# Placing the context branch among the expert weights by order edges on TensorE, and norming the second context at the end of the mixer

## The chip, the cores and the metric

The kernel runs on one core of a Trainium2 chip, in float32 (large products by three passes over a split of the operands). The metric is the device time of one launch in microseconds (us), as a median of runs. The profile is one further execution, with every instruction recorded.

## The reference

Two blocks of two layers each, on a latent sequence x and a context, both 256 tokens of width 1024. The first block mixes the context and the latents (heads with a scan, a convolution, a Fourier mix) and runs 16 experts behind each mixer; the second layer of it does both for the latents alone. The second block starts with a Hyena layer on both sequences and ends with attention on the latents over latents and context. Cut to what the change touches:

```python
# first block, last layer (l = 1): latents only
x = x + gt1 * (mix_x @ w_out[l])
x = x + gt2 * expert_choice_ffn(modulated_rmsnorm(x, g_norm2[l], sh2, sc2), ...)   # 16 experts, 32 tokens each
# second block, layer 0
h_ctx = rms_norm(ctx_2, norm_g) * (1 + sc_c) + sh_c          # needs nothing of the first block
proj = h_ctx @ w_in                                          # 1024 x 8192, four parts: x0, x1, v, z
x0, x1, v = short_conv(proj[..., :6144])                     # width 3
u = x1 * v
y = irfft(rfft(u, 512) * rfft(k, 512))[:256]                 # long convolution, done as products with DFT matrices
x_ctx = ctx_2 + gt_c * (((y + u * d) * x0 * silu(z)) @ w_out)   # 2048 x 1024
```

So the context's Hyena branch of the second block depends on nothing that the second layer's experts compute, and the two can run side by side.

## The kernel before, in words

**Order.** The program is written as one stream of tile operations, and a scheduler with a simulated timeline (`schedule_with_timeline_sim=True` in `build`) fixes the order of the instructions of each engine ahead of the run. An engine then works through its list in order and waits where an operand or a buffer is not ready. What is written in parallel (the experts and the context branch) is interleaved by that scheduler, by the times that it simulates.

**Queues.** SP issues nearly all weight loads: tiles of 128x2048 (1.05 MB) into the tag W with 5 buffers. In `run` the context branch has a ring of its own, the tag Wb with 2 buffers, and its loads are issued by POOL for the first 15 of its 16 tiles (the blocks `(0, 4), (4, 4), (8, 4), (12, 3)`), and by SP for the sixteenth (`[(15, 1)]`), which waits for expert 14 (`self.late[14]`).

**The second layer, in order.** `mixer(1, ...)` ends with the heads' loop (L582 to L608), the Fourier mix (L644), the convolution's norm (L666 to L673) and the output projection: `loadN` (L320) loads w_out in four loads of four k-blocks, `projN_steps` splits each k-block into hi (L104, ScalarE) and lo (L105, VectorE) and multiplies in three passes (L109 to L111). `ada` computes the adaLN vectors, tile by tile: a load (L186), and for each eight matmuls into the bank `pad` (L191). Which adaLN tiles are computed where is the table `PLACES`: in "L1" they are mixed into the heads' loop, one step after every head step (`beside`), in "R1" they come in `route_tokens`, ahead of the gathering of the experts' tokens (L798). The tiles "a1 b0 b1" are the three last groups of the second block's two layers: 16 loads.

**The experts.** `experts` runs for each of 16 experts over gate, up and down weights: each is four tiles of two k-blocks (`ew`, L895), and each k-block is one `expert_k` (L823), with the stationary operand the 32 gathered tokens (XS) or the hidden values (hT) and the weights streaming through. The four quarters of a k-block's 1024 columns go to four groups of 32 rows of the array: 3 x 8 x 4 matmuls for each expert. Between up and down lie ScalarE (L851), VectorE (L854), a transpose (L857) and its copy (hT). VectorE weights the result (L869), and every fourth expert it is scattered back by matmuls (L875). The first six weight tiles go to a tag of their own, W2 (6 buffers; `r = 11 - self.ecount`), all others to W, so that eleven can be loaded ahead of the first expert.

**The context branch.** `hyena` handles 128 channels at a time: for each of the four parts one load of 128x1024x2 and one `projT` of eight k-blocks, split in halves of four (hi, lo in 2 buffers, `sbufs`), 24 matmuls of 256 columns for each. VectorE and ScalarE form the short convolution, POOL folds u into sums and differences (L1058), TensorE transposes them (L1059), goes through the DFT matrix fe and, after VectorE's product with the kernel's spectrum Kt (L1077), back through fi (L1017). The results hm feed `out_proj`, in blocks of four tiles. Before, the context is loaded, its adaLN row and column formed and the normed transposes hyx made at the place where the branch begins, behind the call of `experts`.

In what follows a *piece* is a projection's half: four k-blocks of one `projT`, or one k-block of `out_proj`. The branch's first 15 tiles make 120 + 30 = 150 pieces.

Of the kernel before, what the change touches and what calls it, by code (L numbers as in the profile page):

```python
# [22 lines left out]

SB = 4
# [3 lines left out]
PLACES = dict(P0="", M0="01 02 10", L0="", R0="a0", W1="", P1="11", M1="12", L1="", R1="a1 b0 b1")  # L28
# [3 lines left out]
class K:  # L32
    def __init__(self, ctx, tc, A, out):
# [14 lines left out]
        self.side, self.turn = (None, 1), 0  # L48
        self.wgate, self.late = [], {}

# [56 lines left out]
    def mm3(self, out, l, r, start, stop):  # L107
        mm = self.nc.tensor.matmul
        mm(out, lhsT=l[0], rhs=r[0], start=start, stop=False)  # L109
        mm(out, lhsT=l[0], rhs=r[1], start=False, stop=False)  # L110
        mm(out, lhsT=l[1], rhs=r[0], start=False, stop=stop)  # L111

# [153 lines left out]
    def projT(self, ps, w, x, c0, n):  # L266
        for k0 in range(0, 8, 4):
# [58 lines left out]
    def mixer(self, l, x, hc, cols, R, ada):  # L326
# [8 lines left out]
        with self.pool("nrm", tags=("xh", "xtmp")):  # L335
            for s, src in ((0, hc), (1, x)):
                xh = self.normed(src, "og" if s else "xh", 1)
# [7 lines left out]
        ott = [0, 1, 2, 3] if full else [2, 3]  # L345
        cum = []
# [5 lines left out]
        wg = {}  # L352
# [72 lines left out]
        flo = T([128, 2, 2, 128], "flo")  # L425
        for s in streams:
# [14 lines left out]
            if s in om:  # L441
                Q[s] = self.parts([128, 1, 256], "Q", 2, True)
# [5 lines left out]
            if s in om:  # L448
# [3 lines left out]
                nc.scalar.activation(flo[:, s], pm, AF.Exp, scale=-1.0)  # L452
# [19 lines left out]
        sgc = T([128, 2, 512], "t4k", 2)  # L472
        ypad = T([128, 2, 2, 286], "ypad")
        nc.vector.memset(ypad[:, :, :, 0:15], 0.0)
        nc.vector.memset(ypad[:, :, :, 271:286], 0.0)
        for h in range(2):
            ps = self.P([128, 512])
            self.projT(ps[:, oc0:], chunk(1 + h), X, oc0, on)
            nc.scalar.activation(sgc[:, h, oc0:], ps[:, oc0:], AF.Sigmoid)
        for h in range(2):  # L480
            ps = self.P([128, 512])
            self.projT(ps[:, oc0:], chunk(3 + h), X, oc0, on)
            for s in om:
                nc.vector.tensor_tensor(ypad[:, h, s, 15:271], ps[:, s * 256:s * 256 + 256],
                                        sgc[:, h, s * 256:s * 256 + 256], op=OP.mult)

        cw, cbias = self.colv["cw", l], self.colv["cb", l]
        acc = T([128, 2, 2, 256], "t4k", 2)
        yo = slice(0, 2) if full else slice(1, 2)

        def terms():
            for j in range(31):
                for h in range(2):
                    av, yv = acc[:, h, yo], ypad[:, h, yo, j:j + 256]
# [10 lines left out]
        qT = T([128, 4, 512], "qT")  # L505
# [4 lines left out]
        for h in range(4):  # L510
            ps = self.P([128, 512])
            self.projT(ps[:, oc0:], chunk(9 + h), X, oc0, on)
            self.copy(qT[:, h, oc0:], ps[:, oc0:])
# [9 lines left out]
        fz = T([128, 4, 256], "t4k", 2)  # L523
# [3 lines left out]
        for q, t in enumerate(ott):  # L527
            self.copy(fz[:, t], pss[q])


        og = T([128, 4, 512], "og")
# [3 lines left out]
        for q, t in enumerate(ott):  # L535
            nc.scalar.activation(og[:, t], pss[q], AF.Sigmoid)
            nc.vector.tensor_tensor(og[:, t], og[:, t], ghn, op=OP.mult)
# [32 lines left out]
        mhi = T([128, 8, 512], "mhi", 1, F32R)  # L570
        mlo = T([128, 8, 512], "mlo", 1, F32R)
# [4 lines left out]
        for s in om:  # L576
            hh[s] = T([128, 4, 2, 128], "hh", 2)
            for h in range(4):
                pS = self.P([128, 2, 256])
                c0 = s * 256  # L580
                for t in range(2):
                    nc.tensor.matmul(pS[:, t], lhsT=kT[:, h, c0 + t * 128:c0 + (t + 1) * 128], rhs=qT[:, h, c0:c0 + 256],  # L582
                                     start=True, stop=True)
                for d in range(2):
# [13 lines left out]
                    if s == 1:  # L598
# [5 lines left out]
                        nc.vector.tensor_tensor(qs, qs, qT[:, h, 256:512], op=OP.mult)  # L604
# [12 lines left out]
                    nc.vector.tensor_tensor(rd, rd, flo[:, s, :, r], op=OP.max)  # L617
# [10 lines left out]
            for h in range(4):  # L628
                pt = self.PT([128, 256])
                for t in range(2):  # L630
                    nc.vector.scalar_tensor_tensor(hh[s][:, h, t], hh[s][:, h, t], rsh[:, s, h, t:t + 1],
                                                   og[:, 2 * s + t, h * 128:(h + 1) * 128], op0=OP.mult, op1=OP.mult)
                    nc.tensor.transpose(pt[:, t * 128:(t + 1) * 128], hh[s][:, h, t], self.ident)
                c0 = s * 256
# [4 lines left out]
        for h in range(2):  # L639
            po = self.PT([128, 512])  # L640
            for s in om:
                ps = self.PS([128, 512])
                for t in range(2):
                    nc.tensor.matmul(ps, lhsT=fz[:, 2 * s + t, h * 128:(h + 1) * 128], rhs=fw[:, t], start=(t == 0), stop=(t == 1))  # L644
# [5 lines left out]
            nc.scalar.copy(mhi[:, 6 + h, oc0:], po[:, oc0:])  # L650
# [951 lines left out]
```

## Time and profile before

| | |
|---|---|
| median of 3 runs | 2360.59 us (2359.33 to 2368.23) |
| profiled execution | 2366.99 us, its span 2365.2 us |
| busy share of the span | PE 90%, PEld 61%, DVE 53%, ACT 31%, POOL 8% |
| mean granted clock of TensorE | 0.955 |
| DMA, mean over the span | 281 GB/s, 664.09 MB |

PE is TensorE's matmuls, PEld its weight loads beside them, DVE is VectorE, ACT ScalarE, POOL GpSimd, SP the engine that issues most loads. PEclk is the clock that TensorE was granted, as a share of full speed (2.4 GHz); 0.76 over a stretch is a mixture of the levels 2.4 and 1.2 GHz. TensorE's 90% is a mean over stages: a table of stretches tells in which of them DMA is the full resource and in which TensorE is. A line of waits names the instruction that stood, the last thing that it stood for, and the time; a line of SP's timeline with a long duration and few issues (54.33 us for 16) is SP standing at a load whose buffer is not free yet.

### The profile page before, as it was taken

What the parts mean: (1) busy time and instruction counts of PE and PEld (TensorE: products, weight loads), DVE (VectorE), ACT (ScalarE), POOL (GpSimd) and SP (SyncE); (2) the same over time, 40 slices, a digit from 0 to 9 for tenths busy, and PEclk for the clock granted to TensorE, in tenths of its full rate; (3) what the DMA queues carried; (4) which work ended last, traced back from release to release, by engine and by line L of the source; (5) the groups of instructions that cost most, each with busy time, mean ns of one, the idle gap of its engine ahead of it and who ended that gap; (6) DMA issues with size and microseconds to landing.
All of it is one profiled execution on the core that took longest, in us unless ns stands there. A gap on an engine that the chain in (4) does not pass through costs nothing.

```text
span 2365.2 us, 35049 instructions
## 1 busy us (share of the span) xinstructions
PE 2135.7 (90%) x13966; PEld 1436.1 (61%) x13966; DVE 1250.4 (53%) x2533; ACT 737.5 (31%) x1414; POOL 187.7 (8%) x315
## 2 busy tenths in 40 slices
PE   5999988999999989998799998898777999999998
PEld 3776664343343436864376766665234999979786
DVE  3954444333433337654355555544125878875776
ACT  3323331000000014343233222222013555555665
POOL 1000000011010100000011011100001110100100
PEclk8999999999999999999899999998777999999999
DMA  8247545999999996459799999988996545435320
GB/s 342 99 157 312 204 184 193 413 415 415 414 413 415 414 405 251 137 194 370 295 351 365 372 374 370 351 336 327 421 421 262 185 144 188 168 132 189 126 81 26
DMA packets 129588, 664.09 MB, mean 281 GB/s; under 512 B 12666, under 2 KB 23429, under 8 KB 62352
## 3 DMA queue, kind: packets, MB, share of 16 engines
q1 hardware_dynamic: 115616, 602.89, 66.0%
q0 software_dynamic: 13808, 58.96, 6.6%
q8 instruction: 110, 1.80, 0.3%
q14 instruction: 54, 0.44, 0.1%
HBM read 656.56 MB, written 5.24 MB: 280 GB/s over the span
## 4 chain that ended last, share of the span: by engine, by line
PE 72%; DVE 9%; issue 8%; DMA 7%; ACT 3%; POOL 1%; SPq 0%; DVEq 0%; POOLq 0%; ACTq 0%
PE pmm L823 16%; PE pmm L109 12%; PE pmm L111 11%; PE pmm L110 11%; PE pad L191 3%; PE psm L875 2%; DMA W<-in_w_e_gate 1%; DVE lo L105 1%; DMA W<-in_w_e_up 1%; PE ptp L1017 1%; DMA W<-in_w_ada 1%; PE pmm L798 1%; PE pad L978 1%; DMA W<-in_ada_w 1%; PE ppo L1247 1%
## 5 line engine op out<-in xcount | busy, mean ns | idle before, releaser
L823 PE MATMUL pmm<-W,XS 128*32 128x256 f32 (+1 forms) x3040 | 378.8, 478 | 39.7 <-DMA W<-in_w_e_gate 20.3
L105 DVE TENSOR_TENSOR lo<-W,hi 128x512 fp32r<-128x512 f32 (+1 forms) x420 | 283.7, 680 | 187.1 <-ACT hi L104 184.2
L104 ACT CAST hi<-W 128x512 fp32r<-128x512 f32 (+1 forms) x420 | 255.5, 612 | 352.0 <-PE pmm L110 162.9
L823 PEld LDWEIGHTS pmm<-W,XS 128*32 128x32 f32 (+1 forms) x3040 | 127.0, 123 | 241.3 <-issue 151.1
L823 PE MATMUL pmm<-W,hT 128*32 128x256 f32 (+1 forms) x1536 | 190.1, 483 | 20.2 <-DVE hT L101 8.3
L111 PE MATMUL pmm<-hyx,lo 128*128 128x256 f32 x640 | 191.6, 299 | 10.6 <-DVE lo L105 10.6
L109 PE MATMUL pmm<-hyx,hi 128*128 128x256 f32 x640 | 193.4, 302 | 4.8 <-ACT hi L104 4.8
L110 PE MATMUL pmm<-hyx,hi 128*128 128x256 f32 x640 | 185.8, 290 | 0.0
L105 DVE TENSOR_TENSOR lo<-Wb,hi 128x512 fp32r<-128x512 f32 x160 | 109.4, 692 | 117.3 <-ACT hi L104 116.3
L104 ACT CAST hi<-Wb 128x512 fp32r<-128x512 f32 x160 | 96.8, 619 | 209.4 <-PE pmm L110 138.3
L869 DVE TENSOR_TENSOR Y<-pmm,gt 32x512 f32<-32x512 f32 (+1 forms) x128 | 70.9, 554 | 143.5 <-PE pmm L823 141.8
L109 PE MATMUL pmm<-hyl,hi 128*128 128x256 f32 x512 | 144.5, 283 | 1.7 <-DVE rtmp L697 1.7
L110 PE MATMUL pmm<-hyl,hi 128*128 128x256 f32 x512 | 144.1, 282 | 0.0
L111 PE MATMUL pmm<-hyl,lo 128*128 128x256 f32 x512 | 143.1, 283 | 0.0
L109 PEld LDWEIGHTS pmm<-hyx,hi 128*128 128x128 f32 x640 | 126.6, 198 | 23.7 <-ACT hi L104 16.6
L111 PEld LDWEIGHTS pmm<-hyx,lo 128*128 128x128 f32 x640 | 126.3, 197 | 22.3 <-DVE lo L105 14.1
L823 PEld LDWEIGHTS pmm<-W,hT 128*32 128x32 f32 (+1 forms) x1536 | 65.6, 125 | 117.6 <-issue 68.6
L110 PEld LDWEIGHTS pmm<-hyx,hi 128*128 128x128 f32 x640 | 126.6, 198 | 2.4 <-issue 2.2
L851 ACT ACTIVATE h<-pmm 128x256 f32<-128x256 f32 (+1 forms) x31 | 15.1, 488 | 362.1 <-PE pmm L823 361.9
L191 PE MATMUL pad<-W,cpad 128*32 128x512 f32 x576 | 91.0, 643 | 21.6 <-DMA W<-in_w_ada 16.7
L854 DVE TENSOR_TENSOR h<-h,pmm 128x512 f32<-128x512 f32 (+1 forms) x32 | 17.7, 552 | 171.9 <-ACT h L851 89.5
L109 PEld LDWEIGHTS pmm<-hyl,hi 128*128 128x128 f32 x512 | 97.4, 190 | 3.4 <-issue 1.9
(516 smaller groups left out, 4084.1 us busy)
## 6 DMA issues: line engine op xcount, KB each, us to landing
W<-in_w_e_gate SPq DMA_DIRECT2D x128, 1024.0 KB, 11.2
W<-in_w_e_up SPq DMA_DIRECT2D x128, 1024.0 KB, 11.2
W<-in_w_e_down SPq DMA_DIRECT2D x128, 1024.0 KB, 11.2
W<-in_w_ada SPq DMA_DIRECT2D x48, 1024.0 KB, 6.6
W<-in_hyw SPq DMA_DIRECT2D x32, 1024.0 KB, 5.1
Wb<-in_hyw POOLq DMA_DIRECT2D x30, 1024.0 KB, 8.9
W<-in_ada_w SPq DMA_DIRECT2D x24, 1024.0 KB, 5.2
W<-in_at_w_in SPq DMA_DIRECT2D x16, 1024.0 KB, 5.0
```

Source lines behind the costliest of these rows:

```text
L104: self.nc.scalar.copy(hi, w)
L105: self.nc.vector.tensor_tensor(lo, w, hi.bitcast(F32), op=OP.subtract)
L109: mm(out, lhsT=l[0], rhs=r[0], start=start, stop=False)
L110: mm(out, lhsT=l[0], rhs=r[1], start=False, stop=False)
L111: mm(out, lhsT=l[1], rhs=r[0], start=False, stop=stop)
L191: nc.tensor.matmul(ps[32 * j:32 * j + 32, :], lhsT=self.cpad[:, blk, k0 + k, :], rhs=wt[:, k, j * 512:(j + 1) * 512], start=(k0 + k == 0), ...
L798: nc.tensor.matmul(ps, lhsT=v, rhs=S[s][:, t], start=(t == 0 and q == 0), stop=(t == 1 and q == 1))
L823: self.nc.tensor.matmul(ps[M * j:M * j + M], lhsT=v, rhs=wt[:, j * N:(j + 1) * N], start=(k == 0), stop=(k == 7))
L869: nc.vector.tensor_tensor(Y[s][32 * r:32 * r + 32, c], py[p0:p0 + 32], gt[s][p0:p0 + 32, c], op=OP.mult)
L875: nc.tensor.matmul(ps, lhsT=SgT[s][:, q, t * 128:(t + 1) * 128], rhs=Y[s][:, n * 512:(n + 1) * 512], start=True, stop=True)
L978: nc.tensor.matmul(ps[:, i, f], lhsT=self.fd[:, t, i * 256 + f * 128:i * 256 + (f + 1) * 128], rhs=ab[:, i, t], start=(t == 0), stop=(t == 1))
L1017: self.nc.tensor.matmul(out, lhsT=l[0], rhs=r[0], start=start, stop=stop)
```

## The change

Six edits, one diff:

1. **Order edges.** `place` adds an edge without a semaphore (it binds the scheduler's order on TensorE, and costs the run nothing) from the first matmul of a piece to an expert cluster. `self.clusters` lists, for the second layer, the last matmul of every second k-block of `expert_k`, that is one cluster for each weight tile, 12 for each expert. The k-th piece of the first 15 context tiles may issue only behind cluster int(1.2 k) - 4.
2. **adaLN.** "a1 b0 b1" go from "R1" (in `route_tokens`) to "L1" (beside the heads of the mixer, ahead of w_out).
3. **Second context.** `load_x("ctx_2")`, its adaLN column and `modulated` go from the start of the context branch to the end of the second mixer, with the pool x2 for its transposes.
4. **Experts of the second layer.** The down projection of expert e - 1 is written behind gate and up of expert e (`put_off`); W2 has 4 buffers for 6 and lies on the other side of the memory, so nine prefetch tiles in place of eleven.
5. **Context branch.** Four hi/lo buffers for two; the transposes of uf come a part later; the back end (inverse transform, product, `out_proj`) is written behind the next tile's third part (`pend`, `flush`); the inverse transform makes 128 columns for each half of the spectrum and forms the other 128 positions by a sum and a reversed difference on VectorE (`back`).
6. **Second mixer.** Tiles of the latents alone have half the width (`on` for 512, `len(om)`, `len(ott)`), and the banks of `ps0` are listed in another order.

```diff
+SHARE, LEAD = 1.2, 4
-PLACES = dict(P0="", M0="01 02 10", L0="", R0="a0", W1="", P1="11", M1="12", L1="", R1="a1 b0 b1")
+PLACES = dict(P0="", M0="01 02 10", L0="", R0="a0", W1="", P1="11", M1="12", L1="a1 b0 b1", R1="")
...
+    def place(self, first):
+
+        if self.mixed is None:
+            return
+        i = int(self.mixed * SHARE) - LEAD
+        self.mixed += 1
+        if 0 <= i < len(self.clusters):
+            self.tc.add_manual_dep(first.ins, self.clusters[i].ins.name,
+                                   mybir.DependencyInfo(mybir.DependencyClass.NoSync, mybir.DependencyReason.DATA),
+                                   reason="share")
...
                 kk = k0 + k
-                self.mm3(ps, (hi[:, k], lo[:, k]), (x[0][:, kk, c0:c0 + n], x[1][:, kk, c0:c0 + n]), kk == 0, kk == 7)
+                first = self.mm3(ps, (hi[:, k], lo[:, k]), (x[0][:, kk, c0:c0 + n], x[1][:, kk, c0:c0 + n]), kk == 0, kk == 7)
+                if k == 0:
+                    self.place(first)
...
             for q, tt in enumerate(tts):
                 c = slice(tt * 128, tt * 128 + 128)
-                self.mm3(pss[q], (x[0][:, k, c], x[1][:, k, c]), (hi, lo), start and k == 0, stop and k == nk - 1)
+                first = self.mm3(pss[q], (x[0][:, k, c], x[1][:, k, c]), (hi, lo), start and k == 0, stop and k == nk - 1)
+                if q == 0:
+                    self.place(first)
...
         for j, v in enumerate(l):
-            self.nc.tensor.matmul(ps[M * j:M * j + M], lhsT=v, rhs=wt[:, j * N:(j + 1) * N], start=(k == 0), stop=(k == 7))
+            last = self.nc.tensor.matmul(ps[M * j:M * j + M], lhsT=v, rhs=wt[:, j * N:(j + 1) * N], start=(k == 0), stop=(k == 7))
+        if ns == 1 and k % 2:
+            self.clusters.append(last)
...
+            if put_off and e:
+                down(e - 1, last)
+            last = hv
+            if not put_off:
+                down(e, hv)
+        if put_off:
+            down(15, last)
...
-            r = (self.ecount - 1) % 10 if ns == 2 else 11 - self.ecount
+            r = (self.ecount - 1) % 10 if ns == 2 else 9 - self.ecount
             if ns == 1 and r >= 5:
-                t = self.T([128, 2, 1024], "W2", 6)
+                t = self.T([128, 2, 1024], "W2", 4)
...
-            fe, fi = T([128, 2, 256], "fe"), T([128, 4, 256], "fi")
+            fe, fi = T([128, 2, 256], "fe"), T([128, 4, 128], "fi")
...
+                self.pend.append(lambda Y=Y, x0s=x0s, m=m, i0=G * g - g0: self.back(Y, x0s, m, i0, blocks[0][1]))
+                if three:
+                    self.flush()
+            self.pend.append(lambda m=m, g0=g0, wg=wg: self.out_proj(x, A["hy_w_out_2"][0], m, g0, wg, gt, dma,
+                                                                     wg - G if three and g0 + wg == 16 else 0))
...
+        if len(Y) == 1:
+
+            for c in range(2):
+                for f in range(2):
+                    self.mmx(py[:, 0, c * 128:(c + 1) * 128], [v[:, c, f] for v in Y], [v[:, 2 * c + f] for v in self.fis],
+                             f == 0, f == 1)
...
                     self.mixer(1, x, hc, m1[1], m1[0], ada)
+
+                    c2 = self.load_x("ctx_2", "hc")
+                    a0 = self.modA(b0[1], 1, self.colv["ng", 0], "a1")
+                    X2 = self.modulated(c2, a0, b0[1][:, 0], 1, xh="W", side="left")
...
                         self.wtag, self.wbufs = "Wb", 2
-                        c2 = self.load_x("ctx_2", "hc")
+                        self.sbufs = 4
                         self.hy_consts(False)
-                        a0 = self.modA(b0[1], 1, self.colv["ng", 0], "a1")
                         gtc = self.row_bcast(b0[0][:, 0], 0, 64, 1, "gtc", 1)
-                        X2 = self.modulated(c2, a0, b0[1][:, 0], 1)
...
+                            self.mixed = 0
                             self.hyena(c2, X2, gtc, pool, [(0, 4), (4, 4), (8, 4), (12, 3)], 1, False)
+                            self.mixed = None
```

On SP, from the end of the second mixer to the first expert weights, the order of the loads was this (in_w_ada and in_ada_w are adaLN tiles of the first and the second block, in_w_out the mixer's output projection, in_w_e_up an expert's up weights; x4 is four loads in a row):

```order
L186 DMA W<-in_w_ada 128x2048 x8
L320 DMA W<-in_w_out 128x4x512 x4
L186 DMA W<-in_ada_w 128x2x1024 x4
L186 DMA W<-in_ada_w 128x2048 x8
L186 DMA W<-in_ada_w 128x2x1024 x4
L895 DMA W<-in_w_e_up 128x2048
```

and is now this:

```order
L201 DMA W<-in_w_ada 128x2048 x8
L201 DMA W<-in_ada_w 128x2x1024 x4
L201 DMA W<-in_ada_w 128x2048 x8
L201 DMA W<-in_ada_w 128x2x1024 x4
L339 DMA W<-in_w_out 128x4x512 x4
L926 DMA W<-in_w_e_up 128x2048 x4
```

The 16 adaLN loads went from behind w_out to ahead of it, and expert weights follow on w_out.

On TensorE, the order where the experts run alone was this (XS and hT are the stationary operands of an expert's gate and up, and of its down weights; hyx are the context's transposes, which begin again here with the sixteenth tile, in the last expert):

```order
L823 MATMUL pmm<-W,XS_7295 32x256 x16
L823 MATMUL pmm<-W,XS_7296 32x256 x16
L857 MATMUL ptp<-cf,h_9398 128x128 x2
L823 MATMUL pmm<-W,hT 32x256 x32
L823 MATMUL pmm<-W,XS_7295 32x256 x8
L109 MATMUL pmm<-hyx_9621,hi 128x256
L110 MATMUL pmm<-hyx_9622,hi 128x256
L111 MATMUL pmm<-hyx_9621,lo 128x256
```

and in the mixed stretch it now reads like this, throughout (u and fe are the forward transform):

```order
L113 MATMUL pmm<-hyx_7189,hi 128x256
L114 MATMUL pmm<-hyx_7188,lo 128x256
L1048 MATMUL psm<-u,fe 128x128 x4
L842 MATMUL pmm<-W,hT 32x256 x8
L842 MATMUL pmm<-W,XS_7357 32x256 x8
L112 MATMUL pmm<-hyx_7188,hi 128x256
```

Weight tiles come singly between pieces, about 10 pieces to an expert through expert 15. Before, there were 16 to an expert through expert 11, and none in experts 12 to 14.

## Rows read from the trace of the kernel before

**Rows 1.** Stretches: length; PE, PEld, DVE, ACT, POOL busy (count); PEclk, DMA share, GB/s.

```profile
500.00:800.00 300.00, 280.46 (x1363) 115.46 (x1362) 101.01 (x171) 12.42 (x21) 31.21 (x59) 1.00 1.01 415
1013.00:1052.00 39.00, 35.41 (x223) 24.99 (x223) 24.11 (x91) 18.14 (x55) 1.84 (x2) 0.98 0.42 156
1052.00:1101.70 49.70, 48.41 (x232) 27.01 (x231) 20.23 (x38) 15.00 (x28) 1.46 (x3) 0.95 0.82 301
...
1140.50:1148.80 8.30, 8.30 (x132) 4.31 (x132) 0.69 (x1) 2.29 (x4) 1.68 (x3) 1.00 0.14 34
...
1186.00:1650.00 464.00, 423.53 (x3826) 314.02 (x3830) 245.23 (x484) 131.01 (x253) 45.36 (x79) 0.97 0.92 354
1650.00:1783.00 133.00, 94.53 (x926) 44.95 (x918) 24.31 (x50) 10.09 (x21) 2.31 (x5) 0.76 1.01 421
...
1148.80:1783.00 634.20, 539.90 (x4958) 368.07 (x4958) 278.86 (x552) 149.47 (x290) 51.08 (x90) 0.91 0.94 371
```

**Rows 2.** TensorE's waits, 1186 to 1650, then 1650 to 1783: total, times, longest.

```profile
PE pmm L111 <- DVE lo L105: 10.6, 11, 1.7
...
PE pmm L823 <- DMA W<-in_w_e_up: 1.5, 1, 1.5
...
PE pmm L823 <- DMA W<-in_w_e_up: 13.6, 13, 2.8
PE pmm L823 <- DMA W<-in_w_e_gate: 10.6, 9, 1.5
PE pmm L823 <- DMA W<-in_w_e_down: 4.6, 5, 1.4
PE ptp L857 <- DVE h L854: 3.8, 4, 1.0
```

**Rows 3.** SP's timeline at the seam: start, duration, line, out<-in, number of loads.

```profile
1013.18 6.03 SPq L320 DMA_DIRECT2D W<-in_w_out  x4
1044.47 54.33 SPq L186 DMA_DIRECT2D W<-in_ada_w  x16
...
1107.83 40.45 SPq L895 DMA_DIRECT2D W<-in_w_e_down  x4
```

**Rows 4.** Chain that ended last, seen from 1010 to 1160: start, duration, what.

```profile
1013.18 7.56 DMA W<-in_w_out
...
1044.47 4.81 DMA W<-in_ada_w
...
1059.81 5.01 DMA W<-in_ada_w
...
1081.08 5.69 DMA W<-in_ada_w
...
1090.38 0.99 PE pad L191 x8
...
1147.09 1.75 ACT xh L227 x3
```

**Rows 5.** TensorE's groups, 1186 to 1650: shapes, count, busy, mean ns, idle before.

```profile
L823 PE MATMUL pmm<-W,XS 128*32 128x256 f32 x1260 | 82.6, 385 | 1.5 <-DMA W<-in_w_e_up 1.5
L823 PE MATMUL pmm<-W,hT 128*32 128x256 f32 x640 | 41.2, 384 | 3.1 <-ACT hT L99 2.1 <-DVE hT L101 1.0
L1017 PE MATMUL ptp<-fi,Yf 128*128 128x256 f32 x120 | 34.1, 408 | 3.2 <-DVE Yf L1077 2.0 <-issue 1.2
```

**Rows 6.** POOL's timeline, where the context branch begins.

```profile
1146.49 0.61 POOL L992 DMA_DIRECT2D fe<-in_fe  x1 [40.86 <-PE pmm L823]
```

**Rows 7.** DMA queues, 1340 to 1440: packets, MB, share of 16 engines.

```profile
q1 hardware_dynamic: 3803, 27.75, 72.1%
q0 software_dynamic: 1665, 9.25, 23.4%
```

More of the change, by code (lines that the diff above doesn't have):

```diff
@@ L108, in mm3 @@
         mm = self.nc.tensor.matmul
-        mm(out, lhsT=l[0], rhs=r[0], start=start, stop=False)
+        first = mm(out, lhsT=l[0], rhs=r[0], start=start, stop=False)
         mm(out, lhsT=l[0], rhs=r[1], start=False, stop=False)
         mm(out, lhsT=l[1], rhs=r[0], start=False, stop=stop)
+        return first
+    def place(self, first):
[7 more added lines that the diff above has]
+                                   reason="share")
     def rsqrt(self, out, in_, scale):
@@ L336, in mixer @@
             for s, src in ((0, hc), (1, x)):
-                xh = self.normed(src, "og" if s else "xh", 1)
+                xh = self.normed(src, ("og" if full else "kT") if s else "xh", 1)
                 self.toT(xh, a1, cols[:, 0], s, xhi[:, :, s * 256:s * 256 + 256], xlo[:, :, s * 256:s * 256 + 256],
@@ L345, in mixer @@
         ott = [0, 1, 2, 3] if full else [2, 3]
+        s0 = 0 if full else 1
         cum = []
@@ L1058, in hyena @@
                                     nc.gpsimd.tensor_tensor(uf[:, c], cv[1][:, :128], cv[1][:, 128:][:, ::-1], op=op)
-                                    nc.tensor.transpose(pt[:, c], uf[:, c], self.ident)
-                                self.put([v[:, :, i * 128:(i + 1) * 128] for v in u], pt)
+                                if not three:
+                                    self.flush()
                         else:
@@ L1064, in hyena @@
                             nc.vector.tensor_tensor(x0s[:, i], sg, cv[0], op=OP.mult)
+                        if q == (1 if three else 2):
+                            pt = self.PT([128, 2, 128])
+                            for c in range(2):
+                                nc.tensor.transpose(pt[:, c], uf[:, c], self.ident)
+                            self.put([v[:, :, i * 128:(i + 1) * 128] for v in u], pt)
                 pu = []
@@ new lines, in hyena, with flush, back @@
+            if three:
+                self.flush()
+        self.flush()
+    def flush(self):
+        p, self.pend = self.pend, []
+        for f in p:
+            f()
+    def back(self, Y, x0s, m, i0, width):
+        G = x0s.shape[1]
+        if not m:
+            m += self.parts([128, width, 256], "hm", 1, True)
+        py = self.PT([128, G, 256])
+        if len(Y) == 1:
+            for c in range(2):
+                for f in range(2):
+                    self.mmx(py[:, 0, c * 128:(c + 1) * 128], [v[:, c, f] for v in Y], [v[:, 2 * c + f] for v in self.fis],
+                             f == 0, f == 1)
+            y = self.T([128, 2, 128], "yh", 1)
+            ye = self.T([128, 128], "ye", 1)
+            nc = self.nc
+            nc.scalar.copy(ye, py[:, 0, :128])
+            nc.vector.tensor_tensor(y[:, 0], ye, py[:, 0, 128:], op=OP.add)
+            nc.vector.tensor_tensor(y[:, 1], ye[:, ::-1], py[:, 0, 128:][:, ::-1], op=OP.subtract)
+            y = y.rearrange("p a b -> p (a b)")[:, None]
+        else:
+            for i in range(G):
+                for q in range(4):
+                    c, f = divmod(q, 2)
+                    self.mmx(py[:, i], [v[:, c, f, i * 128:(i + 1) * 128] for v in Y], [v[:, q] for v in self.fis], q == 0, q == 3)
+            y = py
+        self.nc.vector.tensor_tensor(x0s, x0s, y, op=OP.mult)
+        self.split(x0s, *[v[:, i0:i0 + G] for v in m])
```

149 lines of the change are left out of this document (73 added, 76 removed).

## The prediction

> **What bounds the kernel now.** I read the table of stretches first, then TensorE's waits in the two stretches that stand out, then the DMA queues and the chain of waits at the seam ahead of them.
>
> The second layer's experts, with the second block's context branch between them, run from 1140.5 to about 1783 us, 27% of the span. They fall into two halves with different limits. From 1186 to 1650 us TensorE is busy 423.5 of 464 us at clock 0.97, and DMA moves 354 GB/s [rows 1]; the longest reason for TensorE to wait is a VectorE split (10.6 us), and an expert weight only 1.5 us [rows 2]. This half is bound by TensorE. From 1650 to 1783 us DMA is full (share 1.01, 421 GB/s) and TensorE, at clock 0.76, waits 13.6 + 10.6 + 4.6 = 28.8 us for the three expert weights [rows 1, 2]. This half is bound by DMA. The order of instructions shows why: before, 15 of the 16 context tiles are through when expert 11 of 16 ends, with 16 pieces (four k-blocks of a projection) to an expert, and experts 12 to 14 then run alone. So each resource rests while the other is full.
>
> Ahead of this lies a second loss. SP issues w_out at 1013 us, then the 16 adaLN tiles of the second block from 1044 to 1099 us, and only then expert weights [rows 3]. The chain that ends last runs through three of those tiles (4.81 + 5.01 + 5.69 = 15.5 us) and before that through w_out (7.56 us) [rows 4]. From 1140.5 to 1148.8 us DMA moves 34 GB/s [rows 1], since SP stands 40.45 us at the first expert's down weights for want of a buffer [rows 3].
>
> **The change part by part.** The order up to the second layer's mixer is the same on every engine, and from the latent Hyena branch on it is the same but for small swaps; I cost both at nothing (the stretch ahead is the same program, and behind it no tile is added). All terms lie between 1013 and 1783 us.
>
> *Even spacing.* The new edges hold about 10 pieces to each expert through expert 15. What then binds? TensorE first. In 1186 to 1650 us 1260 + 640 = 1900 expert records took 82.6 + 41.2 = 123.8 us, 0.065 us each [rows 5]. The whole stage has 16 x 3 x 8 x 4 matmuls of two records, 3072. TensorE's work there is 423.5 + 1172 x 0.065 = 76 for the rest, + 20 for the sixteenth tile ((423.5 - 123.8) / 15), - 17 because the inverse transform now streams 128 columns where it streamed 256 (34.1 us halved) = 502 us. The waits of the mixed half were 464 - 423.5 = 40.5 us; I keep them, though the deferred back end, four hi/lo buffers for two, and the late down projection (3.8 us waited for h in the tail [rows 2]) should shorten them: 543 us.
>
> DMA next. From 1148.8 to 1783 us it moved 371 GB/s x 634.2 us = 235.3 MB [rows 1]. The amount hardly changes: two fewer prefetch tiles add 2.1 MB; two context tiles, a kernel tile and constants (2.6 MB) come earlier, because the context pool no longer lies over the first expert buffers (POOL's first constant waited 40.86 us for TensorE there [rows 6]). So 235 MB. The rate: alone the SP queue fills the engines at 421 GB/s; with both queues at work, their 27.75 + 9.25 = 37.0 MB took 72.1 + 23.4 = 95.5 us of all 16 engines, 387 GB/s, with 25% of the bytes on POOL's queue [rows 7]. Over the whole stage POOL's queue carries 150 pieces and 15 kernel tiles of 0.262 MB, 43 MB, beside 192 expert tiles of 1.05 MB, 201 MB: 18%. So between the two rates 421 - 34 x 18/25 = 397; I take 395, as a few gaps remain, and 235 / 0.395 = 595 us. That is more than TensorE's 543, so DMA sets the end throughout. Ends: 421 GB/s (558 us) and 380 (618 us). The first layer's experts, with DMA as their limit and TensorE busy 280 of 300 us, ran at 415 GB/s [rows 1]. Against 634.2 us this is -39 us (-76 to -16).
>
> The Trainium skill, on the page DMA: Bandwidth & Descriptors, section Specifications, gives a core's share of HBM as about 358 GB/s. By it the stage would take 235 / 0.358 = 656 us, and spreading would gain nothing. The trace does not agree: 421 GB/s held for 133 us [rows 1].
>
> *adaLN tiles into the heads' loop.* The 16 loads and their 64 matmuls move ahead of w_out on SP and TensorE. DMA has room there (share 0.42 from 1013 to 1052 us [rows 1]). Gone are the waits above: ScalarE no longer stands with w_out's first split in front of the heads' exponentials (7.56 us), nor TensorE on 15.5 us of tiles. New: five W buffers must pass 16 more tiles at 1.05 / 0.421 = 2.5 us each, 40 us from 1013 us, before w_out lands; so w_out arrives near 1060, not 1021, and is used from about 1061, not 1053. Its 96 products need 0.23 us each, 22 us, and took from 1052 to 1101 because a tile's product of 0.99 us or more stood between most steps [rows 4] and the convolution's norm came late. I estimate their end at 1092. Route then loses the products of three last tiles (about 2 us of its chain). So the first expert starts at 1130, not 1140.5: -10 us. From below: the waits return in full (+5); from above: all of 7.6 + 15.5 less 7 us is kept (-16).
>
> *Second context normed early.* Two squares, two scalings, 16 transposes and their copies go from the experts' start to the mixer's end. They hide under w_out's products, where ScalarE is busy 15 and VectorE 20 of 50 us [rows 1]; uncovered, ScalarE's squares alone would hold its splits 1.75 us [rows 4], inside the bounds above. They free the first pieces to run beside expert 0 instead of after 1186 us.
>
> *Prefetch.* Nine tiles instead of eleven (9.4 MB, 22 us at 421) are in before the start, and DMA resumes when the first up weights are used, about 5 us after the start where it was 8.3 us: -3 us. The smaller tiles in the mixer and the new bank order cost no instruction.
>
> Sum: -39 - 10 - 3 = -52 us. The profiled execution took 2366.99 us (span 2365.2), which gives 2315 on its own scale; the median of the three runs is 2360.59, and from there 2308 us.
>
> **Rivals.**
>
> *The mixed rate stays.* Pieces and weights wait for each other, so that the engines never fill, and the rate stays at 371 GB/s: 634 us, only 13 us won, 2348. For: SP has five buffers and the context two, and both queues are fed by engines that wait in order. Against: TensorE's waits in the mixed half were not on DMA [rows 2], so its 354 GB/s was demand, not supply.
>
> *The mixed rate is a ceiling.* If 354 GB/s were all that two queues can draw, 235 MB would take 664 us over the whole stage, + 30 - 13 = + 17 us, 2377. Against: 387 GB/s at full engines with both queues [rows 7]. I give it 2 in 100. The 358 GB/s of the Trainium skill's page DMA: Bandwidth & Descriptors (section Specifications) would make it 656 us and 2370; no stretch with full DMA here was so slow.
>
> *The seam moves instead of going.* TensorE is in order and now has products of adaLN tiles between the heads' steps; if the ring of buffers turns slower than 2.5 us a tile, w_out comes near 1075 and the start stays at 1145 to 1150 us: 18 us lost of the 52, 2326.
>
> *TensorE's clock falls, slower than before.* With DMA as the limit, TensorE has a gap at every weight. In the tail, where that was so, the granted clock was 0.76 [rows 1], that is, much of the time at 1.2 GHz instead of 2.4. If it fell so over the whole stage, 502 x 0.97 / 0.76 = 641 + 40 = 681 us, the stage ends 1135 + 681 = 1816 and the kernel near 2394. It decides against the change from 502 x 0.97 / c + 40 = 648 on, a clock under 0.80. Against: TensorE would be busy 543 of 595 us, and in 1186 to 1650 us, busy 423.5 of 464, it had 0.97 [rows 1].
>
> *More than forecast.* DMA keeps 421 GB/s throughout: 558 us, 89 us won, 2271.
>
> **How the numbers follow.** Forecast 0.60 (own range 2280 to 2331: 415 to 385 GB/s, the start up to 8 us later with the slower rate); mixed rate stays 0.12; ceiling 0.02; seam 0.10; clock 0.08; more 0.08. The likeliest gives 2308. The range 2272 to 2346 leaves out half of "more", half of "rate stays", the ceiling and the clock: 0.20. A half per cent, 11.8 us, is about what a measurement of this kernel can tell from no change. Faster than 2348.8: 0.60 + 0.10 + 0.08 + 0.05 of the 0.12 = 0.83; slower than 2372.4: clock and ceiling, 0.10; the rest, 0.07, is the same.
>
> **What would show it.** After: DMA share near 1.0 from some 10 us behind the first expert to the last weight, with 385 to 421 GB/s and no stretch of weights alone; an expert every 37 to 40 us throughout; TensorE's waits on W spread thinly; clock 0.9 or more; the first expert at 1124 to 1136 us, w_out's waits in place of those on the block's adaLN tiles; last weight near 1730. The forecast is wrong if DMA stays under 375 GB/s with TensorE waiting on hi, lo or uf, if the granted clock is under 0.8, or if the first expert does not start earlier.

## The result, and the profile after

The changed kernel takes 2324.81 us (2322.87 to 2329.89), the kernel before 2362.48 us in the same comparison: a ratio of 0.9841 (95% interval 0.9815 to 0.9867), 38 us. The forecast was 2308 (2272 to 2346). The profiled execution took 2329.89 us, its span 2328.1.

The table of stretches of the changed kernel (columns as in [rows 1]): two in the mixer, the stage of the experts from 8 us behind its start to the last weight's load, and most of that stage alone.

```profile
1001.00:1066.00 65.00, 64.83 (x398) 38.03 (x395) 28.37 (x88) 21.54 (x56) 0.00 (x0) 1.00 0.86 326
1066.00:1118.00 52.00, 47.95 (x202) 32.04 (x200) 29.06 (x62) 23.21 (x47) 4.19 (x7) 0.87 0.57 204
...
1163.00:1744.00 581.00, 511.44 (x4980) 353.60 (x4972) 286.57 (x584) 149.04 (x297) 44.64 (x84) 0.97 1.00 407
...
1250.00:1746.00 496.00, 436.08 (x4310) 295.74 (x4305) 244.80 (x495) 123.27 (x244) 36.59 (x68) 0.98 1.01 414
```

Where [rows 1] had one half at 354 GB/s and one at clock 0.76, the stage now has full DMA (share 1.00, 407 GB/s) and TensorE busy 511 of 581 us at clock 0.97. Its waits, from 1163 to 1744 us (who, for what: us in total, times, longest):

```profile
PE pmm L842 <- DMA W<-in_w_e_gate: 19.4, 12, 4.7
PE pmm L842 <- DMA W<-in_w_e_up: 13.3, 12, 2.0
PE ptp L1048 <- DVE Yf L1112: 9.4, 10, 2.3
PE ptp L1098 <- POOL uf L1088: 6.6, 5, 4.0
PE pmm L842 <- DMA W<-in_w_e_down: 6.1, 7, 1.8
```

Waits for gate and up weights head the list, and the three weights make 38.8 us together, over the whole stage, where [rows 2] had them almost wholly in its last fifth. The marks at which the stretches below begin and end are read from TensorE's timeline (start, duration, line, out<-in, count): the first product of the heads, the last of them, the last of w_out's, the first and the last of the experts, and the first of the latents' projections. A mark is the start of its row, so that a stretch ends 0.4 to 3 us before the last product of it does.

```profile
1003.18 1.02 PE L601 MATMUL pmm<-qT,kT 128*128 128x256 f32 x4
...
1066.19 0.39 PE L631 MATMUL pmm<-C,qs 128*128 128x129 f32 x2
...
1117.62 0.40 PE L114 MATMUL pmm<-hi,mlo 128*128 128x512 f32 x1
...
1154.99 2.37 PE L842 MATMUL pmm<-W,XS 128*32 128x256 f32 x40
...
1752.44 1.93 PE L842 MATMUL pmm<-W,hT 128*32 128x256 f32 x16 [2.33 <-DMA W<-in_w_e_down]
...
1783.41 0.58 PE L112 MATMUL pmm<-hyl,hi 128*128 128x256 f32 x1
```

The same six marks were read from each trace; the columns add up to the span (all in us):

| kernel | up to heads | heads | w_out | routing | experts | to latents | rest | span |
|---|---|---|---|---|---|---|---|---|
| before | 999.3 | 46.1 | 55.1 | 40.0 | 648.4 | 31.7 | 544.7 | 2365.2 |
| changed | 1003.2 | 63.0 | 51.4 | 37.4 | 597.5 | 31.0 | 544.7 | 2328.1 |
| e1: no edges | 996.7 | 63.0 | 50.4 | 37.9 | 657.1 | 29.1 | 544.5 | 2378.7 |
| e2: before + edges | 998.9 | 45.8 | 53.8 | 38.6 | 602.8 | 31.7 | 544.8 | 2316.4 |
| e3: adaLN put back | 999.0 | 46.1 | 56.3 | 43.6 | 600.5 | 30.2 | 543.8 | 2319.5 |
| e4: adaLN and norm put back | 999.1 | 45.9 | 53.9 | 38.5 | 600.5 | 30.9 | 544.7 | 2313.4 |
| e5: norm put back | 1000.8 | 63.0 | 45.8 | 37.1 | 607.0 | 31.6 | 544.3 | 2329.6 |
| e6: e4, full inverse | 1000.7 | 44.9 | 56.0 | 38.5 | 606.8 | 31.7 | 544.7 | 2323.3 |
| e7: e4, half the weights | 1001.8 | 45.0 | 52.9 | 39.8 | 564.6 | 30.8 | 544.6 | 2279.4 |
| e8: e4, prefetch and gate | 999.3 | 47.1 | 56.0 | 38.7 | 600.5 | 29.6 | 545.9 | 2317.0 |

The change took 50.9 us from the experts and gave 10.6 of them back between the heads and the first expert (46.1 + 55.1 + 40.0 = 141.2 before, 151.8 after). Each is one trace: e2, the same program as before up to the first expert, has 138.2 there, and e1, the same as the changed one, 151.3, so the loss is 10 to 14 us. The first column, 3.9 us more, is no part of it: the ten traces lie between 996.7 and 1003.2 there, and e1, which is the same program up to that point, is the lowest of all.

### The profile page after: what moved, and what is told of

Its sections match the earlier page's. It is cut to its first block, busy times and chain, and to the rows that moved or that the text cites. A ratio compares the mean times of both kernels' runs of the same rounds, so it can differ in the third digit from the quotient of the medians.

```text
span 2328.1 us, 35073 instructions
## 1 busy us (share of the span) xinstructions
PE 2116.1 (91%) x13966; PEld 1427.5 (61%) x13966; DVE 1258.1 (54%) x2565; ACT 742.2 (32%) x1430; POOL 184.5 (8%) x315
## 5 line engine op out<-in xcount | busy, mean ns | idle before, releaser
L842 PE MATMUL pmm<-W,XS 128*32 128x256 f32 (+1 forms) x3040 | 368.1, 460 | 34.0 <-DMA W<-in_w_e_gate 20.7
L114 PE MATMUL pmm<-hyx,lo 128*128 128x256 f32 x640 | 184.9, 290 | 1.8 <-DVE lo L108 1.8
L112 PEld LDWEIGHTS pmm<-hyx,hi 128*128 128x128 f32 x640 | 126.0, 197 | 46.6 <-issue 30.9
L206 PE MATMUL pad<-W,cpad 128*32 128x512 f32 x576 | 91.5, 647 | 20.4 <-DMA W<-in_w_ada 17.0
L112 PEld LDWEIGHTS pmm<-hyl,hi 128*128 128x128 f32 x512 | 97.5, 190 | 3.4 <-issue 1.9
L113 PEld LDWEIGHTS pmm<-hyl,hi 128*128 128x128 f32 x512 | 97.4, 190 | 0.0
L114 PEld LDWEIGHTS pmm<-hyl,lo 128*128 128x128 f32 x512 | 96.8, 190 | 0.0
```

The lines of the kernel that those rows point to most:

```text
L112: first = mm(out, lhsT=l[0], rhs=r[0], start=start, stop=False)
L206: nc.tensor.matmul(ps[32 * j:32 * j + 32, :], lhsT=self.cpad[:, blk, k0 + k, :], rhs=wt[:, k, j * 512:(j + 1) * 512], start=(k0 + k == 0), ...
L842: last = self.nc.tensor.matmul(ps[M * j:M * j + M], lhsT=v, rhs=wt[:, j * N:(j + 1) * N], start=(k == 0), stop=(k == 7))
```

## The experiments

**The edges, taken away and added alone.** e1 is the changed kernel without `self.mixed = 0`:

```diff
-                            self.mixed = 0
                             self.hyena(c2, X2, gtc, pool, [(0, 4), (4, 4), (8, 4), (12, 3)], 1, False)
```

> The changed kernel without its order edges on TensorE; all other parts stay. In the order of instructions the context's pieces now stand 16 to 19 to an expert and are through by expert 9; experts 10 to 14 run alone. Theory (even spacing is the gain): a TensorE-bound stretch at some 350 to 370 GB/s, then some 170 us of weights alone at 420 GB/s with the clock under 0.9; the stage is 30 to 45 us longer than in the changed kernel, 2350 to 2370 us. Rival (the gain came from the deferred back end, the half inverse transform and the later down projection): the mixed stretch stays over 400 GB/s and the time within 10 us of the changed kernel, 2320 to 2335 us.

Measured: 2380.25 us, ratio to before 1.0072 (1.0057 to 1.0087). Its stretches:

```profile
1156.00:1620.00 464.00, 415.11 (x3746) 305.62 (x3737) 247.38 (x512) 131.27 (x271) 43.51 (x79) 0.95 0.93 350
1620.00:1797.00 177.00, 127.37 (x1238) 56.66 (x1234) 35.10 (x72) 11.93 (x26) 1.71 (x5) 0.76 1.01 418
```

Without edges the other five edits together are slower than before, and in two places: the seam between the heads and the first expert keeps its loss (151.3 us for 141.2), and the experts take 8.7 us more, since the scheduler packs the context denser, at 350 GB/s, and weights alone at clock 0.76 follow for 177 us (133 before). The time lies 10 us above the range that the theory gave. e2 adds to the kernel before what `place` and `clusters` need, and nothing else:

```diff
+        if ns == 1 and k % 2:
+            self.clusters.append(last)
...
+                if k == 0:
+                    self.place(first)
...
+                            self.mixed = 0
                             self.hyena(c2, X2, gtc, pool, [(0, 4), (4, 4), (8, 4), (12, 3)], 1, False)
+                            self.mixed = None
```

> The kernel before with the order edges alone: about 10 pieces to an expert from expert 4 on, nothing else changed. Theory (even spacing is the gain, and the seam of the changed kernel lost 10 us): the stage runs at 400 to 415 GB/s and loses 40 to 50 us, the first expert starts at 1140 us as before, 2312 to 2325 us. Rival (the edges need the other parts: with two hi/lo buffers, the down projection in its old place and the back end not deferred, TensorE waits on VectorE and ScalarE between weight tiles): 370 to 390 GB/s, 2335 to 2355 us.

Measured: 2319.93 us, 0.9817 (0.9801 to 0.9833), no slower than the whole change. From 8 us behind its first expert to the last weight's load:

```profile
1145.00:1732.00 587.00, 525.95 (x4945) 356.75 (x4938) 278.90 (x551) 151.03 (x289) 51.48 (x90) 0.95 0.99 400
```

So the edges alone give 45.6 of the 50.9 us in the experts, without the seam's loss. The rival's wait is there, h ahead of the down projection 16.6 us, but it costs little while DMA is full:

```profile
PE ptp L877 <- DVE h L874: 16.6, 11, 2.1
PE pmm L841 <- DMA W<-in_w_e_gate: 15.5, 9, 3.0
```

**The two seam edits, each way.** e3 puts `PLACES` back, e4 the norm too, e5 the norm alone:

```diff
-PLACES = dict(P0="", M0="01 02 10", L0="", R0="a0", W1="", P1="11", M1="12", L1="a1 b0 b1", R1="")
+PLACES = dict(P0="", M0="01 02 10", L0="", R0="a0", W1="", P1="11", M1="12", L1="", R1="a1 b0 b1")
...
-                    X2 = self.modulated(c2, a0, b0[1][:, 0], 1, xh="W", side="left")
...
+                        X2 = self.modulated(c2, a0, b0[1][:, 0], 1)
                         with self.pool("bgb") as p:
```

> The changed kernel with the adaLN tiles a1 b0 b1 back behind w_out (PLACES as before); the second context is still normed at the end of the mixer. In the changed kernel's trace the first expert starts at 1155 us, 14.5 us later than before (3.9 us of that already at the heads' loop). Theory (the move put 17 us of adaLN products into a heads' loop in which TensorE was the full engine, and took less out behind it): the first expert at 1143 to 1149 us, the time 6 to 12 us shorter than the changed kernel, 2313 to 2319 us. Rival (it is the second context's norm that delays the start): the first expert stays at 1153 us or later and the time within 4 us of the changed kernel.

> The changed kernel with both seam edits undone: adaLN tiles back behind w_out and the second context loaded and normed behind the call of the experts; edges and all else stay. Theory (the adaLN move is the loss, the early norm about free): the first expert at 1141 to 1146 us, and the first pieces one expert later, which the full DMA hides: 2311 to 2319 us, within 4 us of the run with adaLN alone put back. Rival one (the early norm is the loss): faster than that run by 5 to 10 us. Rival two (pieces that start one expert later leave DMA unfilled at the start and crowd TensorE afterwards): 2322 to 2335 us.

> The changed kernel with the second context normed behind the call of the experts, as before; the adaLN tiles stay in the heads' loop. From the start of the heads' loop to the first expert it took 141 us before, 151.8 in the changed kernel, 146.0 with the adaLN tiles put back, and 138.2 with both seam edits undone. Theory (the two losses of the seam add up, 6 us by the adaLN tiles and 8 by the norm): 144 us from the heads to the first expert, the time 2319 to 2324 us. Rival (the norm costs only where the adaLN tiles crowd it, or the adaLN tiles cost only beside the norm): 138 to 140 us and 2315 us, or 150 us and 2326 us.

Measured: e3 2320.81 us, 0.9819 (0.9804 to 0.9833); e4 2315.69, 0.9796 (0.9781 to 0.9810); e5 2331.45, 0.9858 (0.9845 to 0.9872). Each edit loses when the other is undone: e4 is faster than e3 by 5 us (its slowest run took 2317.39, e3's fastest 2320.16) and than e5 by more (their intervals are apart). Undoing one alone is not told from the changed kernel by time, as the intervals of e3 and of e5 overlap its own. The first expert of e3 comes at 1145.0 us as the theory had it, though its time missed the range by 2 us; and e4 is 5 us faster still, as its first rival had it. From the heads' start to the first expert it takes 138.3 us in e4, 145.9 with the adaLN move alone (e5), 146.0 with the early norm alone (e3), 151.8 with both. The eight traces with both undone (e4, and e6 to e12 below) lie between 137.6 and 141.8, so each edit costs 4 to 8 us there, and both 10 to 14. e5's time missed its range, since its experts took 607 us where e3 and e4 have 600.5 and the changed kernel 597.5; why is open.

What each loses is on TensorE. The heads' loop of the changed kernel, grouped by line (busy us, mean ns, idle before), and that of before behind it:

```profile
L206 PE MATMUL pad<-W,cpad 128*32 128x512 f32 x148 | 23.4, 601 | 0.0
L628 PE MATMUL pmm<-va,t2k 128*128 128x129 f32 x63 | 9.6, 276 | 0.0
...
L608 PE MATMUL pmm<-va,t2k 128*128 128x129 f32 x61 | 9.2, 275 | 0.0
L191 PE MATMUL pad<-W,cpad 128*32 128x512 f32 x48 | 6.4, 605 | 0.0
```

adaLN products took 23.4 us in the loop where they had taken 6.4, and the loop became 17 us longer, the same 17: TensorE had no room there before:

```profile
999.00:1045.00 46.00, 45.09 (x279) 31.89 (x278) 26.55 (x85) 21.15 (x57) 0.00 (x0) 1.00 0.57 220
```

Behind the loop the 17 us don't come back: w_out and routing shrink by 9.5 us only (e5 against e4), since w_out's products cannot close up. In the changed kernel they begin among the heads' last transposes (L653) and break off, from 1089 to 1098 us, until the convolution's norm is through (L693):

```profile
1079.49 0.66 PE L653 MATMUL ptp<-cf,hh 128*128 128x128 f32 x2 [1.26 <-DVE mlo L656]
1079.80 1.20 PE L112 MATMUL pmm<-hi,mhi 128*128 128x512 f32 x2
...
1088.46 0.81 PE L114 MATMUL pmm<-hi,mlo 128*128 128x512 f32 x2
...
1093.96 1.22 PE L693 MATMUL psm<-cf,rc 128*128 128x128 f32 x4 [0.35 <-POOL rc L136]
...
1098.46 1.12 PE L112 MATMUL pmm<-hi,mhi 128*128 128x512 f32 x1
```

In e4 they break off as well, from 1064 to 1075 us, but adaLN products stand in the gap. The stretches of w_out and of routing, first of e4, then of e5:

```profile
1045.40:1099.30 53.90, 49.83 (x239) 26.05 (x237) 22.90 (x48) 16.10 (x33) 3.29 (x5) 0.97 0.79 290
1099.30:1137.30 38.00, 27.33 (x132) 15.36 (x131) 22.44 (x58) 12.85 (x21) 2.83 (x5) 0.87 0.72 291
...
1064.20:1109.90 45.70, 42.10 (x180) 27.73 (x178) 23.12 (x50) 17.04 (x35) 3.29 (x5) 0.93 0.62 227
1109.90:1146.70 36.80, 21.54 (x90) 13.85 (x91) 21.67 (x55) 13.00 (x21) 2.82 (x5) 0.77 0.38 150
```

TensorE's busy time falls by 13.5 us (77.2 to 63.6), not by 17, and its idle time rises by 4 us. The 3.5 us between are an estimate of what the lower clock took from the products that stayed, 0.93 and 0.77 in e5 for 0.97 and 0.87 in e4. The early norm loses differently. It takes a W buffer ahead of the adaLN tiles, whose loads begin 14.8 us later in e3 than in e4:

```profile
1058.88 44.38 SPq L201 DMA_DIRECT2D W<-in_ada_w  x15
...
1044.06 53.12 SPq L201 DMA_DIRECT2D W<-in_ada_w  x16
```

So their last products land among the router's (L747), which are clear of them in e4:

```profile
1111.99 3.63 PE L206 MATMUL pad<-W,cpad 128*32 128x512 f32 x16 [1.36 <-DVE adbC L215]
1115.45 1.06 PE L747 MATMUL psm<-S,wr 128*32 128x256 f32 x8
1116.32 1.45 PE L206 MATMUL pad<-W,cpad 128*32 128x512 f32 x5
```

Routing takes 43.6 us in place of 38.5, and what the norm should have brought, pieces beside the first expert, changes nothing in the experts (600.5 in both). Between the changed kernel and e5, which differ in the norm alone too, the experts do differ, 597.5 against 607.0, and that is the open point above.

**What sets the end of the experts.** Both runs start from e4. e6 gives TensorE more work, e7 gives DMA less (its second and fourth parts use the first and third part's weights).

```diff
-            fe, fi = T([128, 2, 256], "fe"), T([128, 4, 128], "fi")
+            fe, fi = T([128, 2, 256], "fe"), T([128, 4, 256], "fi")
...
-        if len(Y) == 1:
+        if len(Y) == 0:
```

> Both seam edits undone, and the context's inverse transform again streams all 256 columns (17 us more of TensorE's work in the stage, and fewer steps on ScalarE and VectorE). Theory (DMA sets the end of the stage): within 4 us of the run with the seam edits undone, 2312 to 2320 us. Rival (TensorE, with its waits, sets the end): 10 to 17 us longer, 2326 to 2333 us.

```diff
-                            wt = self.W([128, 2, 8, 128])
+                            nw = 2 if three or gate is not None else 1
+                            wt = self.W([128, nw, 8, 128])
...
-                        self.projT(ps, wt[:, q % 2], X, 0, 256)
+                        self.projT(ps, wt[:, q % nw], X, 0, 256)
```

> Both seam edits undone, and in the first 15 context tiles one half of the projections' weights is loaded and used twice: the second and the fourth part are computed with the first and the third part's weights, so 15.7 MB less are moved and TensorE's work is the same. Theory (DMA sets the end of the stage): 15.7 MB at 0.41 MB/us are 38 us, until TensorE takes over at some 555 us; the stage 550 to 562 us where it was 592, the time 2274 to 2288 us. Rival (TensorE with its waits sets the end already, and DMA is only just full): less than 15 us, 2301 us or more.

Measured: e6 2323.48 us, 0.9824 (0.9809 to 0.9839); e7 2282.62 us, 0.9651 (0.9634 to 0.9668). Their stretches in the experts, e6 and then e7:

```profile
1148.00:1741.00 593.00, 527.52 (x5016) 359.40 (x5010) 284.02 (x562) 148.13 (x289) 45.82 (x84) 0.96 1.00 401
...
1147.00:1698.00 551.00, 504.19 (x5020) 348.08 (x5014) 289.66 (x594) 152.10 (x305) 46.29 (x84) 0.98 1.00 403
```

In e7, 15.7 MB less take 35.9 us from the experts, of the 38 that they weigh, and DMA is full as before. So DMA sets the end. But TensorE is close behind: in e6 the experts take 6.3 us more than in e4 (606.8 us, where e4 and e8 to e12 lie between 599.5 and 600.6). What was added is less than the 17 us that the expectation reckoned with, as the inverse transform's rows say, e4 and then e6:

```profile
L1048 PE MATMUL ptp<-fi,Yf 128*128 128x128 f32 x128 | 21.1, 288 | 8.4 <-DVE Yf L1112 7.4 <-PE pmm L842 0.6
...
L1048 PE MATMUL ptp<-fi,Yf 128*128 128x256 f32 x128 | 33.1, 389 | 5.7 <-DVE Yf L1112 5.1 <-PE pmm L842 0.6
```

That is 12 us more work for 6.3 us more time, between the theory and its rival; the time missed the theory's range by 3.5 us. Work on the second resource costs here about half of what it weighs; e6 also has fewer steps on ScalarE and VectorE, which were not separated from it.

**A version that beats both.** e4 does, and was then varied. e8 has eleven prefetch tiles and lets expert 15 release the sixteenth tile; e9 has the prefetch alone, e10 folds u on VectorE, e11 does e9's and e10's edits, e12 is e10 with 1.1 clusters to a piece.

```diff
-            r = (self.ecount - 1) % 10 if ns == 2 else 9 - self.ecount
+            r = (self.ecount - 1) % 10 if ns == 2 else 11 - self.ecount
...
-                            self.hyena(c2, X2, gtc, sync, [(15, 1)], 1, False, self.late[14])
+                            self.hyena(c2, X2, gtc, sync, [(15, 1)], 1, False, self.late[15])
...
-                                    nc.gpsimd.tensor_tensor(uf[:, c], cv[1][:, :128], cv[1][:, 128:][:, ::-1], op=op)
+                                    (nc.gpsimd if three else nc.vector).tensor_tensor(uf[:, c], cv[1][:, :128], cv[1][:, 128:][:, ::-1], op=op)
...
-SHARE, LEAD = 1.2, 4
+SHARE, LEAD = 1.1, 4
```

> A version to beat both: the seam edits undone, eleven prefetch tiles in place of nine (W2 with six buffers, as before), and the sixteenth context tile's weights released by expert 15 where expert 14 released them, so that it fills TensorE's idle stretch behind the last expert weight. Theory: 2.1 MB less to move in the stage (5 us) and two weight tiles and the tile's spectrum behind the last expert weight (3 to 7 us): 2303 to 2309 us. Rival (the sixteenth tile's matmuls then stand ahead of the first latent tile, which is next on the path): 2316 us or more.

> Both seam edits undone, eleven prefetch tiles in place of nine and the sixteenth tile released by expert 14 as in the changed kernel; this is the first half of the run that changed both. Theory: the stage loses what the two tiles weigh, 2.1 MB or 5 us, and the stretch behind the last expert weight stays at 584 us: 2309 to 2313 us. Rival (the start of the experts comes later, as in the run that changed both, by 3.6 us from the heads' loop on, and takes the gain back): 2314 to 2318 us.

> Both seam edits undone, and in the context branch VectorE folds u into sums and differences, where POOL did (32 operations of 0.45 us). TensorE waited 9.0 us for POOL's result in that stage, up to 4.0 us at a time. Theory (DMA sets the end, TensorE close behind it, as the full inverse showed: 17 us more of TensorE's work cost 8): 2 to 5 us faster than with POOL, 2310 to 2314 us. Rival (TensorE waits elsewhere instead, VectorE has more to do): within 2 us, or slower.

> Both seam edits undone, with eleven prefetch tiles and the fold on VectorE. If the two gains are there and add up: 2305 to 2310 us. If either is not there: as the other alone.

> As the run with the fold on VectorE, but with 1.1 clusters to a piece in place of 1.2: the order has 11 pieces to an expert and is through with the 15 tiles one expert earlier. Theory (the spacing must match the demand of both resources, and one expert alone costs only where TensorE then idles): 0 to 6 us slower than with 1.2. Rival (the end of the stage is what counts, and an earlier end of the context leaves TensorE free for the sixteenth tile): 2 to 5 us faster.

Measured: e8 2318.23 us, 0.9793 (0.9777 to 0.9808); e9 2315.60, 0.9799 (0.9778 to 0.9819); e10 2313.03, 0.9780 (0.9760 to 0.9800); e11 2318.81, 0.9809 (0.9789 to 0.9828); e12 2315.78, 0.9794 (0.9774 to 0.9813). All intervals overlap e4's: none of the four edits is told from nothing, so that a time inside an expected range (e10, e12) confirms nothing either. In e8 the last weight's load is issued at 1720 us where e4 has 1730, but the experts take 600.5 us as before, because the sixteenth tile's products now stand among the last down products in TensorE's order. e9's two more tiles ahead of the start left the experts at 600.6 us; why they gain nothing is open, as its rival's reason, a start 3.6 us later, is not there (1138.3 us, 1137.3 in e4). In e10 the wait for uf went to VectorE (7.8 us) instead of POOL (9.0), as its rival had it. The best measured is e4, with or without the fold on VectorE: 2313 to 2316 us, and e4's interval (0.9781 to 0.9810) lies below that of the change (0.9815 to 0.9867).

## Why the prediction was right or wrong

The time was inside the range, and inside the likeliest case's own range (2280 to 2331), but two terms were off in opposite directions: the experts gave 9 us more than forecast, the seam took 21 us more. That one hid a part of the other was luck.

*Even spacing: right in mechanism, short in size.* Forecast -42 us (-39, and -3 for DMA's earlier restart), measured -50.9. The -3 did not come: DMA moved 104 GB/s over the first 8 us and was full only behind them, as before. The amount was right (235 MB forecast; 407 GB/s over 581 us are 236.5). The rate was not: 395 forecast, 407 measured, 414 over 496 us. The step that failed is the reading of [rows 7]: I divided 37.0 MB by the packets' 95.5 us and took the 387 GB/s for what a mixture of two queues can draw, with POOL's queue as the slower part. In the changed kernel, from 1250 to 1740 us, the two queues show this (packets, MB, share of 16 engines):

```profile
q1 hardware_dynamic: 23486, 168.63, 83.6%
q0 software_dynamic: 6064, 33.66, 16.8%
```

That is 168.63 / (0.836 x 490) = 412 and 33.66 / (0.168 x 490) = 409 GB/s: here the queues are alike. [rows 7] gives 385 and 395 for them, in a stretch in which DMA was not quite full (95.5%).

*DMA sets the end, TensorE 50 us behind it: the first is shown by e7, the margin was too large.* e7 shows that TensorE can follow at least 36 us, and e6 that work added to it costs half its length already. TensorE's work was forecast at 502 us for the stage and is 524 busy from the first expert's product to the last. One term is known: -17 for the half inverse transform, taken as half of 34.1 us, is -12 (21.1 us against 33.1).

*The seam: wrong.* Forecast -10, measured +10.6. The failed step is "DMA has room there": the row that I read for it [rows 1, the stretch from 1013 to 1052] shows TensorE busy 35.4 of 39 us, and its own line should have been costed. The sum moved 64 matmuls, four to a tile (eight records in the trace), at no cost; the loop's rows show 100 records more and 17 us, laid on the engine that was full. I had put the cost of the loads through the W ring there, and nothing for the products. The ring was mis-sized too: forecast were 2.5 us a tile and w_out's first product at 1061 us. SP took 48.04 us for the 16 tiles, 3.0 us each, w_out was issued from 1065.6 us on, and its first product stands at 1079.8 (1075.9 without the first column's 3.9 us):

```profile
1017.02 48.04 SPq L201 DMA_DIRECT2D W<-in_ada_w  x16
1065.55 9.04 SPq L339 DMA_DIRECT2D W<-in_w_out  x4
...
SPq L201 <- PE pad L206: 27.8, 10, 7.1
```

27.8 of the 48 us SP stood for buffers that TensorE's adaLN products (L206) had not yet freed: the ring turned at the pace of the full engine. The second failed step is that the norm's steps "hide under w_out's products", argued from ScalarE's and VectorE's room: its cost lies on TensorE and in the order of the adaLN tiles behind it, 4 to 8 us (e3 against e4 and the other traces with both edits undone).

*Rivals.* "The seam moves" named 2326 us and the first expert at 1145 to 1150. The first expert came at 1155, 1151 without the 3.9 us of the first column, and the time was 2324.81. The sign that it named came: the ring turned at 3.0 us a tile, and w_out, 7 to 10 us in landing, came near 1075 us. But DMA did not slow the ring, as TensorE waited for none of the second block's adaLN tiles in the changed kernel; TensorE's full loop did. That the time came so close is chance in part, since the experts gave more than that rival reckoned with. "The mixed rate is a ceiling" and "the mixed rate stays" fell with 407 GB/s. The 358 GB/s that the Trainium skill gives as a core's share of HBM (DMA: Bandwidth & Descriptors, section Specifications) were no limit to this core, with 414 held for 496 us. "The clock falls" did not come in the experts (0.97); it came in w_out's stretch (0.87 from 1066 to 1118 us), where nobody had looked for it.

*What was left out.* e2 shows what the prediction never separated: that one of the six edits carries the gain, and that it needs none of the others.

## What to carry to other kernels

Where two streams with different limits run side by side in a scheduler's order, look for stretches in which one resource rests while the other is full; binding one stream's steps to the other's progress by edges without semaphores removed most of them here, and what was left to win was set first by the fuller resource; the other one's work still cost half its length. Before work is moved to "where there is room", read the row of the engine that executes it and not of the queue that feeds it. Undo each part of a bundle by itself: here one part carried the gain, and two of the others cost 10 to 14 us together.

## What had not been expected of the hardware

DMA's rate in packet time differed between two mixed stretches with packets of the same size (7.2 to 7.3 KB on SP's queue, 5.6 on POOL's): 385 and 395 GB/s where DMA was not quite full [rows 7], 412 and 409 in the filled stage, with both queues in use each time. Being full is not all of it. In e7 from 1250 to 1680 us, and in the kernel before from 500 to 800 us, DMA was full too:

```profile
q1 hardware_dynamic: 21544, 154.53, 87.8%
q0 software_dynamic: 5671, 20.62, 12.3%
...
q1 hardware_dynamic: 16325, 118.87, 96.5%
q0 software_dynamic: 2544, 5.32, 4.7%
```

SP's queue has 409 and 411 GB/s there, POOL's 390 and 377, with packets of 3.6 and 2.1 KB. Which of the two, fullness or size, does what was not tried by itself.

And taking work away from TensorE beside w_out was followed by a lower clock. In the changed kernel TensorE had gaps in one stretch beside w_out and was granted 0.50 (1.2 GHz) in the next, while it had work throughout:

```profile
1075.00:1080.00 5.00, 3.32 (x21) 1.88 (x18) 2.26 (x5) 3.48 (x7) 0.89 (x2) 0.86 1.05 387
1080.00:1085.00 5.00, 5.00 (x13) 3.81 (x13) 3.08 (x6) 0.99 (x2) 0.00 (x0) 0.50 0.33 122
```

So the work that was left took longer: w_out's products of 512 columns start 0.43 us apart at 1081 us and 0.23 us apart at 1086. That the gaps brought the clock down is read from the rows and was not tried by itself.
